# The second half of one transformer layer put into one written order, from the last output projection group to the final norm

## The chip, the cores and the metric

One core of a Trainium2 chip runs the whole kernel in one launch. The metric is the device time of one execution in microseconds (us); less is better. All data are fp32, and a product of high accuracy is made from three products of split operands.

## What is computed

One layer of a diffusion backbone over 512 latent tokens and 256 context tokens with 2048 features. Only the parts around the change matter here. `mod_x` gives six vectors per feature (shift, scale and gate for each of the two blocks):

```python
x = x + g1 * (_merge_heads(o_da, o_mla, subln_w[l], lambda_init) @ w_o[l])
h2 = _modulate(_rmsnorm(x, norm2_w[l]), sh2, s2)
x = x + g2 * _conv_ffn(h2, w_up[l], conv_w[l], conv_b[l], w_down[l])
...
return _rmsnorm(x, final_w)

def _conv_ffn(h, w_up, conv_w, conv_b, w_down):
    g, u = jnp.split(h @ w_up, 2, axis=-1)
    T = g.shape[1]
    gp = jnp.pad(g, ((0, 0), (pad, pad), (0, 0)))
    g = sum(gp[:, j:j + T] * conv_w[j] for j in range(CONV_W)) + conv_b
    return (jax.nn.silu(g) * u) @ w_down
```

## The kernel before

Activations lie with features on the 128 partitions and the 512 tokens along the free dimension: 16 tiles of 128 features. Every operand is split into a high part (cast on ACT) and a low part (raw minus high, on DVE); `mm3` makes a product from three matmuls (L101). A weight block is 128 x 1024 floats: its raw tile `wr` is loaded from the SyncE queue, its high part is `wh`, its low part `wl`, three buffers each.

**Output projection** (L690 to L715). Four groups `g` of four feature tiles, eight weight blocks each, 24 matmuls of 512 columns per block. The 16 products that give the gate of the second block (`next_gemv`) are issued in the groups 1 to 3. After a group DVE adds the residual (L711), the sum `x1` goes to memory from the POOL queue (L714), ACT squares it and POOL adds the squares up in `ss` (L673, L674) for all but the last four tiles.

**Second norm and first two tiles** (L735 to L796). `token_norm` sums the squares over the partitions with matmuls against ones (L680, L684), takes the logarithm and the exponential (L159, L160) and four DVE operations (L161 to L164). Then `first_pair` makes two gate and two up tiles in eight jobs of two feature tiles: `normed` scales a tile (L747), ACT adds the shift per token half (L751), DVE makes the low half (L752). `classical` uses each half on its own: 48 matmuls of 256 columns per weight block. Beside this, `sums` (L756 to L773) makes four sums of quadrants on DVE and splits each into high and low for the later products. This stage has no order written by hand: a scheduler places its operations in each engine's list.

**Third tile, Strassen products and output blocks** (L878 to L1065). From here on the order of PE, ACT, DVE and SyncE is the order of the program (`manual_schedule`). The list `jobs` holds four jobs `u` for the third tile, then seven products `p` per later tile, with the output blocks `d` between them; a job casts and splits the block two jobs ahead. Weight blocks come through two `Ring` objects of three buffers (`wr` and `rb`); a ring issues the next load when a buffer's last use is written.

**Last output block and final norm** (L1069 to L1085). Again placed by the scheduler: for each token half the last four tiles of the activation are multiplied with eight weight blocks (`down`), 24 matmuls of 256 columns each; DVE adds the residual (L843), ACT squares, POOL adds up. When both halves are done, each half has its `token_norm`, then 16 scales on DVE (L1084) and 16 stores from the SyncE queue (L1085).

Of the kernel before, what the change touches and what calls it, by code (L numbers as in the profile page):

```python
# [17 lines left out]
P = 128  # L18
# [34 lines left out]
def layer_kernel(ctx: ExitStack, tc: tile.TileContext, small, rope, c_row, cc_row, x_t, ctx_t, ada, ada_k,  # L53
# [601 lines left out]
    HT = T // 2  # L655
# [20 lines left out]
    def token_norm(pool, ss, last):  # L676

        n = ss.shape[1]
        po = b_tile()[:, :n]
        pe.matmul(po, ones32, ss, start=True, stop=False)  # L680
        for i, x in enumerate(last):
            q = pool.tile([P, T], F32, tag="h", name=nm("sq"), bufs=5)[:, :n]
            sc.square(q, x)
            pe.matmul(po, ones32, q, start=False, stop=i == len(last) - 1)  # L684
        r = pool.tile([P, T], F32, tag="nr", name=nm("nr"), bufs=1)[:, :n]
        t1, t2 = (pool.tile([P, T], F32, tag="h", name=nm("n"), bufs=5)[:, :n] for _ in range(2))
        rstd(r, po, D, t1, t2)
        return r

    x1, ss = [], wo.tile([P, T], F32, name="ss")  # L690
    gv = iter([80 + i for i in range(16)])
    for g in range(4):
# [5 lines left out]
        for kb in range(8):  # L698
            if g and kb % 4 != 3:
                next_gemv(wo, 1)  # L700
            wh, wl = wblock(w_o[g, kb])
            order = [(j, i) for j in range(2) for i in range(4)]
            for j, i in sorted(order, key=lambda t: t[1]) if kb == 7 else order:
                kt, o = kb * 2 + j, j * 512 + i * P
                mm3(outs[i], (wh[:, o:o + P], wl[:, o:o + P]), osp[kt], kt == 0, kt == 15)
        for i in range(4):
            dt = g * 4 + i
            xr = wo.tile([P, T], F32, tag="xr", name=nm("xr"), bufs=3)
            nc.sync.dma_start(xr, x_t[dt])
            x = b2k()  # L710
            ve.scalar_tensor_tensor(out=x, in0=outs[i], scalar=modx[:, 32 + dt:33 + dt], in1=xr,  # L711
                                    op0=ALU.mult, op1=ALU.add)
            x1.append(x)
            gp.dma_start(x1_d[dt], x)  # L714
            if g < 3:  # L715
                add_square(wo, ss, x, dt == 0)
    for dt in range(KT):
        ve.scalar_tensor_tensor(out=a2[:, dt:dt + 1], in0=modx[:, 64 + dt:65 + dt], scalar=1.0,
                                in1=col("n2", dt), op0=ALU.add, op1=ALU.mult)
    db = sm.tile([P, 8], F32, name="db")  # L720
    ve.tensor_tensor(db, modx[:, 56:64], modx[:, 48:56], op=ALU.add)
    wo.release()
    ps_b.release()
    ps_s.release()
    nb[0] = 3
    ps_b = ctx.enter_context(tc.tile_pool(name="ps_m", bufs=4, space=PSUM, reuse_waits="tile"))
# [5 lines left out]
    ff = tc.alloc_tile_pool(name="ff", bufs=1, reuse_waits="tile")  # L732
    hp = tc.alloc_tile_pool(name="hp", bufs=1, side="right", reuse_waits="tile")
    h0, h1 = slice(0, HT), slice(HT, T)
    r = token_norm(hp, ss, x1[12:])  # L735

    def half(t):
        return t[:, h0], t[:, h1]


    hf, hx, t1, t2, t3, t4 = ([None] * KT for _ in range(6))

    def normed(kt):

        b = modx[:, 48 + kt:49 + kt]
        h = hf[kt] = hp.tile([P, T], F32, tag="h", name=nm("h"), bufs=5)
        ve.scalar_tensor_tensor(out=h, in0=x1[kt], scalar=a2[:, kt:kt + 1], in1=r, op0=ALU.mult, op1=ALU.mult)  # L747
        hx[kt] = (a2k(F32R), a2k(F32R) if kt >= 8 else hp.tile([P, T], F32R, tag="h12", name=nm("h12"), bufs=8))
# [31 lines left out]
    def first_pair():  # L780
# [13 lines left out]
        for j in (6, 7):  # L794
            sums(j)
# [374 lines left out]
```

## Time and profile before

| | |
|---|---|
| three runs, us | 2471.26, 2473.78, 2473.87 (median 2473.78) |
| the profiled execution, us | 2470.59 |
| its span, first to last instruction, us | 2468.8 |
| mean granted clock of PE | 0.987 |
| busy share of PE, weight loads, DVE, ACT, POOL | 97%, 81%, 70%, 45%, 10% |
| the chain that ended last | PE 75%, DVE 14%, DMA 4%, ACT 4%, issue 3%, POOL 1% |

The table tells where the time of the whole span lies; a stage may have another limit than the span. In a timeline a line has its start, its length in us, the engine, the line of the program, the operation, output and inputs by name, and the count of merged instructions; in brackets stands how long the engine was idle before it and what ended that. SPq is the SyncE queue, which issues loads and stores. A matmul's length is longer than the distance to the next one, since matmuls overlap.

### The profile page before, as it was taken

Reading aid. Unit: us, or ns where it says so; the run is one execution under the profiler, and the core shown is the slowest. Engines: PE = TensorE matmul, PEld = TensorE weight load, DVE = VectorE, ACT = ScalarE, POOL = GpSimd, SP = SyncE. Lnnn points to the kernel's source line nnn. Section 1 sums busy time; section 2 is a strip of 40 time slices with the busy share of each in tenths; the row PEclk is TensorE's granted clock in tenths of the full one; section 3 lists DMA queues with packets and bytes.
Section 4 is the critical chain, followed back from the end, with each engine's and each line's share of the span. In section 5 each row is a group of like instructions: output and inputs, shape, how many; then the busy total and the mean of one; then the engine's idle time right before and its main releaser. Section 6 shows DMA issues by size and latency. Waiting matters only on the chain.

```text
span 2468.8 us, 33004 instructions
## 1 busy us (share of the span) xinstructions
PE 2388.4 (97%) x12796; PEld 1987.7 (81%) x12796; DVE 1731.8 (70%) x2274; ACT 1117.2 (45%) x1668; POOL 243.4 (10%) x266
## 2 busy tenths in 40 slices
PE   7999999999999999999999999999999999999996
PEld 3778878777677778888888888888888888888886
DVE  4668786398968777387676767675757575757576
ACT  4343121165645542254454545454545454545443
POOL 0000000121200002100101010101010101010113
PEclk8999999999999999999999999999999999999998
DMA  7868889554411158423656465655555555555664
GB/s 274 282 226 307 323 329 321 195 153 131 123 58 43 44 210 314 137 82 119 146 128 146 129 144 130 144 131 142 132 142 135 139 135 139 135 138 136 137 180 145
DMA packets 131859, 407.51 MB, mean 165 GB/s; under 512 B 14451, under 2 KB 25203, under 8 KB 123251
## 3 DMA queue, kind: packets, MB, share of 16 engines
q1 hardware_dynamic: 106422, 356.11, 44.5%
q0 software_dynamic: 25280, 49.30, 11.5%
q8 instruction: 100, 1.64, 0.3%
q14 instruction: 57, 0.47, 0.1%
HBM read 335.88 MB, written 69.48 MB: 164 GB/s over the span
## 4 chain that ended last, share of the span: by engine, by line
PE 75%; DVE 14%; DMA 4%; ACT 4%; issue 3%; POOL 1%; SPq 0%; ACTq 0%; DVEq 0%; POOLq 0%
PE y L981 9%; PE b L104 9%; PE b L105 9%; PE b L106 9%; PE z L981 5%; PE y L982 5%; PE s L104 3%; PE s L105 3%; PE s L106 3%; DMA ada<-in_ada 3%; DVE wl L957 3%; PE s L482 3%; PE z L982 2%; PE x L981 2%; ACT wh L951 1%
## 5 line engine op out<-in xcount | busy, mean ns | idle before, releaser
L104 PE MATMUL b<-ah,wh 128*128 128x512 f32 (+1 forms) x768 | 288.1, 376 | 3.9 <-ACT ah L823 3.9
L105 PE MATMUL b<-al,wh 128*128 128x512 f32 (+1 forms) x768 | 287.0, 374 | 0.0
L106 PE MATMUL b<-ah,wl 128*128 128x512 f32 (+1 forms) x768 | 287.0, 374 | 0.0
L1001 POOL DMA_DIRECT2D x_d<-xs x160 | 139.7, 1004 | 1173.4 <-ACT xs L1000 1171.4
L80 ACT CAST wh<-wr 128x1024 fp32r<-128x1024 f32 (+2 forms) x134 | 132.5, 989 | 269.6 <-PE b L106 78.6
L957 DVE TENSOR_TENSOR wl<-wr,wh 128x1024 fp32r<-128x1024 f32 x125 | 152.7, 1222 | 116.1 <-ACT wh L951 116.1
L981 PE MATMUL y<-a2k,wh 128*128 128x512 f32 x656 | 233.6, 398 | 0.0
L951 ACT CAST wh<-wr 128x1024 fp32r<-128x1024 f32 x125 | 131.3, 1051 | 216.0 <-PE b L105 85.9
L957 DVE TENSOR_TENSOR wl<-rb,wh 128x1024 fp32r<-128x1024 f32 x123 | 150.2, 1222 | 110.6 <-ACT wh L951 110.3
L957 DVE TENSOR_TENSOR wl<-ws,wh 128x1024 fp32r<-128x1024 f32 x123 | 150.2, 1221 | 109.5 <-ACT wh L951 109.4
L81 DVE TENSOR_TENSOR wl<-wr,wh 128x1024 fp32r<-128x1024 f32 (+2 forms) x134 | 155.9, 1164 | 100.9 <-ACT wh L80 97.3
L951 ACT CAST wh<-rb 128x1024 fp32r<-128x1024 f32 x123 | 129.4, 1052 | 203.2 <-PE b L105 58.4
L951 ACT CAST wh<-ws 128x1024 fp32r<-128x1024 f32 x123 | 128.9, 1048 | 154.6 <-DVE ws L925 65.8
L171 DVE CUSTOM_DVE_ANT_0 ada<-ada,cb,smt 128x2048 f32<-128x2048 f32 x64 | 150.6, 2354 | 64.1 <-DMA ada<-in_ada 64.0
L982 PE MATMUL y<-a2k,wl 128*128 128x256 f32 x656 | 183.9, 280 | 0.0
L104 PEld LDWEIGHTS b<-ah,wh 128*128 128x128 f32 x768 | 145.6, 190 | 30.4 <-ACT ah L823 4.1
L106 PEld LDWEIGHTS b<-ah,wl 128*128 128x128 f32 x768 | 145.8, 190 | 26.7
L105 PEld LDWEIGHTS b<-al,wh 128*128 128x128 f32 x768 | 146.0, 190 | 22.6
L981 PE MATMUL y<-b2k,wh 128*128 128x512 f32 x410 | 148.1, 398 | 0.0
L981 PEld LDWEIGHTS y<-a2k,wh 128*128 128x128 f32 x656 | 123.2, 188 | 30.4
L104 PE MATMUL b<-a2k,wh 128*128 128x512 f32 (+1 forms) x376 | 139.8, 374 | 6.6 <-ACT a2k L751 5.0
L105 PE MATMUL b<-a2k,wh 128*128 128x512 f32 (+1 forms) x376 | 140.4, 374 | 0.4 <-DVE a2k L752 0.4
(368 smaller groups left out, 6111.7 us busy)
## 6 DMA issues: line engine op xcount, KB each, us to landing
ada<-in_ada SPq DMA_DIRECT2D x64, 1024.0 KB, 7.0
rb<-in_w_up SPq DMA_DIRECT2D x123, 512.0 KB, 4.5
wr<-in_w_dn SPq DMA_DIRECT2D x96, 512.0 KB, 4.2
x_d<-xs POOLq DMA_DIRECT2D x160, 256.0 KB, 6.0
wr<-in_w_up SPq DMA_DIRECT2D x53, 512.0 KB, 4.1
wr<-in_w_f SPq DMA_DIRECT2D x34, 512.0 KB, 6.9
adak<-in_ada_k SPq DMA_DIRECT2D x32, 512.0 KB, 6.2
ada<-in_ada SPq DMA_DIRECT2D x32, 512.0 KB, 6.4
```

The costliest lines, as they stand in the source:

```text
L80: sc.copy(dst_h, src)
L81: ve.tensor_tensor(dst_l, src, dst_h.bitcast(F32), op=ALU.subtract)
L104: pe.matmul(out, st[0], mv[0], start=start, stop=False, **kw)
L105: pe.matmul(out, st[0], mv[1], start=False, stop=False, **kw)
L106: pe.matmul(out, st[1], mv[0], start=False, stop=stop, **kw)
L171: ve.tensor_tensor_reduce(out=junk, in0=w, in1=vec, op0=ALU.mult, op1=ALU.add, scale=1.0, scalar=col("b_ada", j), accum_out=dst[:, j:j + 1])
L482: pe.matmul(s[:, c0:c1], a, b[:, c0:c1], start=i == 0, stop=i == len(mms) - 1)
L951: sc.copy(hi, raw)
L957: ve.tensor_tensor(lo, raw, hi.bitcast(F32), op=ALU.subtract)
L981: pe.matmul(o, w[j][0], hs[j], start=start and j == 0, stop=False, skip_group_check=True)
L982: pe.matmul(o[:, h0], w[j][1], hs[j][:, h0], start=False, stop=j == 7, skip_group_check=True)
L1001: gp.dma_start(x1_d[dt], x, accum_op=ALU.add)
```

## The change

The order written by hand now begins at the last of the four groups of the output projection and ends with the last store. `jobs` gets eight jobs `o` (last group), eight jobs `n` (the first two tiles) in front and sixteen jobs `f` (last output block, two token halves) behind; all weight blocks but those of `rb` come through one ring.

In `last_projection` the last group's four tiles end one after the other; three of the five sum matmuls stand between the projection's matmuls, and the norm's chain runs by token halves. In `first_tiles` PE takes both feature tiles of a block for the first token half, then for the second; the next block's two tiles are scaled, then the block two ahead is cast and split; every second job POOL forms the quadrant sums in place (four adds per pair of tiles), and ACT and DVE split them at once, in front of the next job's work. `after` issues what `act_after` and `vec_after` issued. In the last stage the two first blocks leave out the last activation tile until it is there; the residual is loaded in one go after the last product; the first half's norm runs beside the second half's matmuls, and in the second half's scaling every third tile goes over ACT and POOL.

```diff
--- before.py
+++ after.py
-    def token_norm(pool, ss, last):
...
+    def residual(dt):
+        xr = wo.tile([P, T], F32, tag="xr", name=nm("xr"), bufs=4)
+        nc.sync.dma_start(xr, x_t[dt])
+        x1.append(b2k())
+        return xr
+    def gated(dt, po, xr, c=slice(0, T)):
+        ve.scalar_tensor_tensor(out=x1[dt][:, c], in0=po[:, c], scalar=modx[:, 32 + dt:33 + dt], in1=xr[:, c],
+                                op0=ALU.mult, op1=ALU.add)
-    for g in range(4):
+    for g in range(3):
...
-            if g and kb % 4 != 3:
+            if g:
                 next_gemv(wo, 1)
...
+    KBS = [kb for j in range(4) for kb in (j, j + 4)]
+    jobs = [("o", kb) for kb in range(8)] + [("n", kb) for kb in KBS] + [("u", b) for b in range(4)]
+    for ft in range(3, NFT):
+        for k in range(7):
+            jobs.append(("p", ft, k))
+            c, n_ = ft // FC, (ft % FC) * 7 + k
+            if c and n_ in DOWN_AFTER:
+                jobs.append(("d", c - 1, DOWN_AFTER.index(n_)))
+    jobs += [("f", th, dp) for th in range(2) for dp in range(8)]
...
+    def high_low(t, src, b=None):
+        hh, hl = half(t)
+        if b is None:
+            sc.copy(hh, src)
+            ve.tensor_tensor(hl, src, hh.bitcast(F32), op=ALU.subtract)
+        else:
+            sc.activation(hh, src, AF.Identity, bias=b)
+            ve.scalar_tensor_tensor(out=hl, in0=src, scalar=b, in1=hh.bitcast(F32), op0=ALU.add, op1=ALU.subtract)
+    def norm_tiles(kt):
+        hf[kt] = mem["hp"].tile([P, T], F32, tag="h", name=nm("h"), bufs=6)
+        hx[kt] = (a2k(F32R), a2k(F32R) if kt >= 8 else mem["hp"].tile([P, T], F32R, tag="h12", name=nm("h12"), bufs=8))
+    def normed(kt, cs=(slice(0, T),)):
+        for c in cs:
+            ve.scalar_tensor_tensor(out=hf[kt][:, c], in0=x1[kt][:, c], scalar=a2[:, kt:kt + 1], in1=mem["r"][:, c],
+                                    op0=ALU.mult, op1=ALU.mult)
+            for t, s in zip(hx[kt], halves):
+                if c.start <= s.start < c.stop:
+                    high_low(t, hf[kt][:, s], modx[:, 48 + kt:49 + kt])
+    def sums(j):
+        a, c = hf[j], hf[j + 8]
+        t1[j] = a2k(F32R)
+        for t in (t3, t2, t4):
+            t[j] = spare.pop(0) if spare else b2k(F32R)
+        d1, d2, d3, d4 = c[:, h1], a[:, h0], a[:, h1], c[:, h0]
+        gp.tensor_tensor(out=d1, in0=c[:, h1], in1=a[:, h1], op=ALU.add)
+        gp.tensor_tensor(out=d3, in0=a[:, h0], in1=a[:, h1], op=ALU.subtract)
+        gp.tensor_tensor(out=d2, in0=d1, in1=a[:, h0], op=ALU.subtract)
+        gp.tensor_tensor(out=d4, in0=c[:, h0], in1=d2, op=ALU.subtract)
+        return [lambda: high_low(t1[j], d1, db[:, j:j + 1]), lambda: high_low(t3[j], d3),
+                lambda: high_low(t2[j], d2, modx[:, 56 + j:57 + j]), lambda: high_low(t4[j], d4)]
...
+    def last_projection(i):
+        kb, w = jobs[i][1], ready[i]
+        if kb < 6:
+            for j in range(2):
+                for d in range(4):
+                    project(live["o"], d, kb * 2 + j, w)
+            cast(i + 2)
+            low(i + 2)
+            return
+        outs, xr = live["o"], live["xr"]
+        def both(d, kbs=(6, 7)):
+            for k in kbs:
+                for kt in (2 * k, 2 * k + 1):
+                    project(outs, d, kt, ready[i - kb + k])
+        def square(src, c=slice(0, T)):
+            if c.start == 0:
+                live["q"] = wo.tile([P, T], F32, tag="sq", name=nm("sq"), bufs=2)
+            sc.square(live["q"][:, c], src[:, c])
+            return live["q"]
+        def put(d):
+            gated(12 + d, outs[d], xr[d])
+            gp.dma_start(x1_d[12 + d], x1[12 + d])
+            return square(x1[12 + d])
+        if kb == 6:
+            both(0)
+            both(1)
+            cast(i + 2)
+            low(i + 2)
+            live["q0"] = put(0)
+            return
+        s = s_tile()
+        po = s[:, :T]
+        both(2)
+        q1 = put(1)
+        pe.matmul(po, ones32, ss, start=True, stop=False, skip_group_check=True)
+        pe.matmul(po, ones32, live["q0"], start=False, stop=False, skip_group_check=True)
+        both(3, (6,))
+        pe.matmul(po, ones32, q1, start=False, stop=False, skip_group_check=True)
+        both(3, (7,))
+        q2 = put(2)
+        pe.matmul(po, ones32, q2, start=False, stop=False, skip_group_check=True)
+        for c in halves:
+            gated(15, outs[3], xr[3], c)
+            q3 = square(x1[15], c)
+            pe.matmul(po[:, c], ones32, q3[:, c], start=False, stop=True, skip_group_check=True)
+        gp.dma_start(x1_d[15], x1[15])
+        wo.release()
+        hp = mem["hp"] = tc.alloc_tile_pool(name="hp", bufs=1, side="right", reuse_waits="tile")
+        r = mem["r"] = hp.tile([P, T], F32, name="nr")
+        n1, n2 = (hp.tile([P, T], F32, tag="h", name=nm("n"), bufs=6) for _ in range(2))
+        for c in halves:
+            sc.activation(r[:, c], po[:, c], AF.Ln, bias=epst, scale=1.0 / D)
+            sc.activation(r[:, c], r[:, c], AF.Exp, scale=-0.5)
+            ve.tensor_scalar(out=n1[:, c], in0=po[:, c], scalar1=1.0 / D, scalar2=EPS, op0=ALU.mult, op1=ALU.add)
+        norm_tiles(0)
+        norm_tiles(1)
+        for c in halves:
+            ve.scalar_tensor_tensor(out=n2[:, c], in0=r[:, c], scalar=-0.5, in1=r[:, c], op0=ALU.mult, op1=ALU.mult)
+            ve.tensor_tensor(n2[:, c], n2[:, c], n1[:, c], op=ALU.mult)
+            ve.scalar_tensor_tensor(out=r[:, c], in0=n2[:, c], scalar=1.5, in1=r[:, c], op0=ALU.add, op1=ALU.mult)
+            for kt in (0, 1):
+                normed(kt, (c,))
+        cast(i + 2)
+        low(i + 2)
+    queue = []
+    def first_tiles(i):
+        kb, n_ = jobs[i][1], KBS.index(jobs[i][1])
+        w = weights(i)
+        if n_ == 0:
+            live["n"] = [b_tile(*t) for t in (("b", 3), ("b", 3), ("x", 1), ("b", 3))]
+        for c in range(2):
+            for j in range(2):
+                for d in range(4):
+                    classical(live["n"][d], kb * 2 + j, w[j * 4 + d], n_ == 0 and j == 0, n_ == 7 and j == 1, (c,))
+        if n_ < 7:
+            for j in range(2):
+                norm_tiles(KBS[n_ + 1] * 2 + j)
+                normed(KBS[n_ + 1] * 2 + j)
+        cast(i + 2)
+        low(i + 2)
+        if n_ % 2:
+            for j in (n_ - 1, n_):
+                queue.extend(sums(j))
+        while queue and n_ < 7:
+            queue.pop(0)()
+    def third_tile(i):
+        b, w = jobs[i][1], weights(i)
+        if b == 0:
+            live["s"] = [b_tile(g_, 2) for g_ in "yz"]
+        for j in range(8):
+            kt = (b % 2) * 8 + j
+            classical(live["s"][b // 2], kt, w[j], kt == 0, kt == KT - 1)
+        while queue:
+            queue.pop(0)()
+        if b == 2:
+            mem["hp"].release()
+            mem["mm"] = tc.alloc_tile_pool(name="mm", bufs=1, side="right", reuse_waits="tile")
+            mem["rb"] = Ring(mem["mm"], "rb", 3, items_b)
+        if b == 3:
+            weight_sum(3, 1)
+        cast(i + 2)
+        low(i + 2)
+        if b < 2:
+            acts[b] = activate(b, live["n"][2 * b], live["n"][2 * b + 1])
...
-        def act_after(i):
...
-        def vec_after(i):
...
+    def after(job):
...
+    def load_residual():
+        for dt in range(KT):
+            x1[dt] = b2k()
+            nc.sync.dma_start(x1[dt], x1_d[dt])
+    rest = []
+    def last_output(i):
+        th, dp = jobs[i][1:]
+        c, n_ = halves[th], th * 8 + dp
+        outs = live.setdefault("f", {})
+        def part(i, fs):
+            w, dp = weights(i), jobs[i][2]
+            for d in range(2):
+                dt = dp * 2 + d
+                if 0 in fs:
+                    outs[dt] = b_tile() if dp != 1 or th else b_tile("xyz"[d], (1, 2)[d])
+                for f in fs:
+                    mm3(outs[dt][:, h0], w[f * 2 + d], [a[:, c] for a in acts[NFT - FC + f]], f == 0, f == FC - 1)
+        if n_ == 0:
+            part(0 + i, (0, 1, 2))
+            part(1 + i, (0, 1, 2))
+            after(jobs[i - 1])
+            v = live[NFT - 1]
+            silu(convolve(NFT - 1, v["g"], v["t"]))
+            acts[NFT - 1] = finish(v["t"], multiply(v["t"], v["u"]))
+            exp_ln_tables()
+        elif n_ == 1:
+            part(i - 1, (3,))
+            part(i, (3,))
+        else:
+            part(i, (0, 1, 2, 3))
+        if n_ == 10:
+            norm_sum(0)
+        cast(i + 2)
+        if n_ > 1:
+            add(n_ - 1 if n_ > 2 else 0)
+            if n_ == 2:
+                add(1)
+        low(i + 2)
+        if n_ == 11:
+            norm_scale(0)
+        if n_ > 11:
+            for _ in range(2 if n_ < 14 else 6):
+                if rest:
+                    rest.pop(0)()
+        if n_ == 15:
+            add(15)
+            norm_sum(1)
+            norm_scale(1)
+            while rest:
+                rest.pop(0)()
...
+    def norm_sum(th):
+        po = live["po", th] = b_tile("y", 2)[:, :HT]
+        for i, q in enumerate((live["ss", th], live["q", th, 0], live["q", th, 1])):
+            pe.matmul(po, ones32, q, start=i == 0, stop=i == 2)
+    def norm_scale(th):
+        r, n1, n2 = fin(), fin(), fin()
+        rstd(r, live["po", th], D, n1, n2)
+        for dt in range(KT):
+            x = x1[dt][:, halves[th]]
+            def scaled(dt=dt, x=x):
+                if th and dt % 3 == 2:
+                    y = fin()
+                    sc.mul(y, x, col("fw", dt))
+                    gp.tensor_tensor(out=y, in0=y, in1=r, op=ALU.mult)
+                else:
+                    y = x
+                    ve.scalar_tensor_tensor(out=y, in0=x, scalar=col("fw", dt), in1=r, op0=ALU.mult, op1=ALU.mult)
+                nc.sync.dma_start(out_t[dt][:, halves[th]], y)
+            rest.append(scaled)
...
+        mem["ra"] = Ring(wp, "wr", 3, items_a)
+        live["o"] = [b_tile() for _ in range(4)]
+        live["xr"] = [residual(12 + d) for d in range(4)]
+        for i in range(2):
+            cast(i)
+            low(i)
         for i, job in enumerate(jobs):
...
+            {"o": last_projection, "n": first_tiles, "u": third_tile, "p": strassen, "d": strassen,
+             "f": last_output}[job[0]](i)
```

## Rows read from the trace of the kernel before

**Rows 1.** The page, busy us, share of the span and instructions of each engine.

```profile
PE 2388.4 (97%) x12796; PEld 1987.7 (81%) x12796; DVE 1731.8 (70%) x2274; ACT 1117.2 (45%) x1668; POOL 243.4 (10%) x266
```

**Rows 2.** Windows, first two tiles: length, each engine's busy time, clock, DMA share, GB/s.

```profile
1080.00:1090.00 10.00, 10.00 (x86) 10.00 (x85) 9.89 (x21) 5.99 (x13) 0.00 (x0) 1.00 0.34 105
```

**Rows 3.** Timeline of PE, from the last projection matmul to the first Strassen product.

```profile
1051.33 0.40 PE L106 MATMUL b<-a2k,wl 128*128 128x512 f32 x1
...
1053.15 3.70 PE L684 MATMUL b<-sq,ones 128*128 128x512 f32 x8 [0.57 <-ACT sq L683]
...
1061.88 0.80 PE L104 MATMUL b<-a2k,wh 128*128 128x256 f32 x2 [5.03 <-ACT a2k L751]
...
1130.98 0.39 PE L104 MATMUL z<-a2k,wh 128*128 128x256 f32 x1 [2.64 <-ACT wh L951]
...
1132.62 0.42 PE L104 MATMUL z<-a2k,wh 128*128 128x256 f32 x1
...
1138.17 0.39 PE L106 MATMUL z<-a2k,wl 128*128 128x256 f32 x1
...
1140.56 0.40 PE L981 MATMUL y<-a2k,wh 128*128 128x512 f32 x1
```

**Rows 4.** Waits of the SyncE queue: waited for, us in total, times, longest.

```profile
SPq L868 <- DVE d L771: 23.0, 1, 23.0
```

**Rows 5.** Timeline of PE, last output block: first, first after the wait, last.

```profile
2391.65 0.28 PE L104 MATMUL b<-ah,wh 128*128 128x256 f32 x1
...
2398.95 1.01 PE L104 MATMUL b<-ah,wh 128*128 128x256 f32 x3 [3.90 <-ACT ah L823]
...
2444.40 0.28 PE L106 MATMUL b<-ah,wl 128*128 128x256 f32 x1
```

**Rows 6.** Timeline of DVE and ACT: the first tile, and the final norm's half.

```profile
1060.53 1.41 DVE L747 SCALAR_TENSOR_TENSOR h<-b2k,a,nr 128x512 f32<-128x512 f32 x2
1061.32 0.51 ACT L751 ACTIVATE a2k<-h,modx 128x256 fp32r<-128x256 f32 x1 [3.08 <-DVE h L747]
...
1061.86 0.48 DVE L752 SCALAR_TENSOR_TENSOR a2k<-h,modx,a2k 128x256 fp32r<-128x256 f32 x1
...
2446.87 0.47 ACT L159 ACTIVATE nr<-b,epst 128x256 f32<-128x256 f32 x1 [6.87 <-PE b L684]
...
2449.21 6.42 DVE L1084 SCALAR_TENSOR_TENSOR b2k<-a2k,smt,nr 128x256 f32<-128x256 f32 x16
```

**Rows 7.** Timeline of ACT and DVE: cast and split of one weight block, low halves of sums.

```profile
1046.09 1.05 ACT L80 CAST wh<-wr 128x1024 fp32r<-128x1024 f32 x1 [4.38 <-PE b L105]
...
1047.17 1.23 DVE L81 TENSOR_TENSOR wl<-wr,wh 128x1024 fp32r<-128x1024 f32 x1 [4.22 <-ACT wh L80]
...
1113.48 0.76 DVE L81 TENSOR_TENSOR b2k<-d,b2k 128x256 fp32r<-128x256 f32 x2
```

**Rows 8.** Timelines of POOL and DVE where adds and weight splits meet or don't.

```profile
2407.14 0.74 POOL L674 TENSOR_TENSOR ss<-ss,sq 128x256 f32<-128x256 f32 x1 [0.44 <-ACT sq L673]
...
2404.88 1.23 DVE L81 TENSOR_TENSOR wl<-wr,wh 128x1024 fp32r<-128x1024 f32 x1 [0.38 <-ACT wh L80]
...
2405.31 1.39 POOL L674 TENSOR_TENSOR ss<-ss,sq 128x256 f32<-128x256 f32 x1 [0.89 <-ACT sq L673]
...
975.40 1.30 POOL L674 TENSOR_TENSOR ss<-ss,sq 128x512 f32<-128x512 f32 x1
...
976.09 1.71 DVE L81 TENSOR_TENSOR wl<-wr,wh 128x1024 fp32r<-128x1024 f32 x1 [1.70 <-ACT wh L80]
```

**Rows 9.** Timeline of ACT: the last gate's operation, and the table load of the final norm.

```profile
2394.41 0.82 ACT L805 ACTIVATE t<-g,smt 128x512 f32<-128x512 f32 x1 [1.36 <-DVE g L1024]
...
2437.70 1.28 ACT L155 ACT_TABLE_LOAD   x1
```

**Rows 10.** Line 1085, the stores: shortest, median, longest ns; us to landing.

```profile
L1085 SPq DMA_DIRECT2D out_t<-b2k x32: 332/408/461, 2449.7 to 2466.0; - x32
...
DMA to landing us min/median/max: 1.7/1.8/2.0
```

More of the change, by code (lines that the diff above doesn't have):

```diff
@@ L720, in layer_kernel @@
[L720 to L748, printed above, removed]
-        for t, c in zip(hx[kt], (h0, h1)):
-            hh, hl = half(t)
-            sc.activation(hh, h[:, c], AF.Identity, bias=b)
-            ve.scalar_tensor_tensor(out=hl, in0=h[:, c], scalar=b, in1=hh.bitcast(F32), op0=ALU.add, op1=ALU.subtract)
@@ L854, in layer_kernel @@
+    items_a, items_b = [], []
+    for job in jobs:
+        if job[0] != "p":
+            items_a.append((job, sources[job[0]](*job[1:]), 1))
+        elif job[2] == 0:
+            ft = job[1]
+            items_a.append((("w11", ft), w_up[ft - 2, 0, 0], 2))
+            items_b += [(("w12", ft), w_up[ft - 2, 1, 0], 2), (("w21", ft), w_up[ft - 2, 0, 1], 2),
+                        (("w22", ft), w_up[ft - 2, 1, 1], 3)]
     class Ring:
@@ new lines, in classical, with activate, gate_in @@
+    def classical(out, kt, w, start, stop, cs=(0, 1)):
+        for i in cs:
+            mm3(out[:, halves[i]], w, half(hx[kt][i]), start and i == 0, stop and i == 1, True)
+    def activate(ft, g, u):
+        t = silu(convolve(ft, g, gate_in(ft, g)))
+        return finish(t, multiply(t, u))
+    def gate_in(ft, g):
+        t = mem["ff"].tile([P, T], F32, tag="t", name=nm("t"), bufs=1)
+        sc.activation(t, g, AF.Identity, scale=col("cw", NFT + ft), bias=col("cb", ft))
+        return t
@@ new lines, in operand, with cast @@
+    def operand(job):
+        ra = mem["ra"]
+        if job[0] != "p":
+            return ra.tiles[job], lambda: ra.used(job)
+        ft, k = job[1:]
+        if k == 0:
+            return ra.tiles["w11", ft], lambda: ra.used(("w11", ft))
+        if k in (2, 3, 6):
+            return sums_[ft, 1 if k == 3 else 2], None
+        key = ({1: "w21", 4: "w12", 5: "w22"}[k], ft)
+        return mem["rb"].tiles[key], lambda: mem["rb"].used(key)
+    def cast(i):
+        if i < last:
+            raw, done = operand(jobs[i])
+            hi, lo = (wp.tile([P, 1024], F32R, tag=g, name=nm(g), bufs=3) for g in ("wh", "wl"))
+            sc.copy(hi, raw)
+            ready[i] = hi, lo, raw, done
```

471 lines of the change are left out of this document (177 added, 294 removed).

## The prediction

> **What bounds the kernel now.** I read the page's busy times first: TensorE (PE) is busy for 97% of the span [rows 1]. The whole change can therefore win back no more than the places where PE stands still or runs at the lower clock, so I looked for those next, in the stretches of ten microseconds after the output projection. One of them, twenty microseconds after the second norm, shows the opposite of what I looked for: PE is busy for all of it and VectorE (DVE) for 9.89 of 10 [rows 2]. A matmul of 256 columns, 0.28 long and counted at both edges, begins there every (10 + 0.28)/86 = 0.12 us. DVE works there at PE's own pace; it has nothing to spare.
>
> Then the timeline of PE alone. The last matmul of the output projection starts at 1051.33 and ends about 0.22 later; call that end E. The first matmul of the up projection starts at 1061.88, 10.3 us after E, and waits 5.03 for ScalarE (ACT). At 1130.98 PE waits again, 2.64, for a weight block, and from 1132.62 to 1138.17 it starts 27 matmuls 0.213 apart, which is the 1.2 GHz level after the 0.12 of the 2.4 GHz level. The first Strassen product starts at 1140.56, 89.0 after E [rows 3]. The late wait comes from the SyncE queue: its loads stood 23.0 us behind the three `rb` loads, whose memory DVE was still reading [rows 4]. The last output block starts at 2391.65, loses 3.90 to the last `ah`, ends at 2444.52 [rows 5], and the remaining 24.3 us to the end of the span are the final norm. So from the last product to the end the kernel needs 77.2 us.
>
> **The change part by part.** Between the first and the last Strassen product the list of instructions is the same (the merged `after` issues what `act_after` and `vec_after` issued, in the same order): 0. The modulation products of the output projection move into its second and third group; both versions load 16 of them beside PE work, so I take 0 there too.
>
> *From E to the first product.* Three of the five sum matmuls go in front of E. Eight records of such sums take 3.70, two per matmul, 0.93 each [rows 3]: E comes 2.8 later. Behind it now stands a chain in token halves. Add and square of 256 columns (0.48 and about 0.4) and half a sum (0.46) end at 1.5. From the logarithm to the first scale the final norm's half takes 2.34 now (2446.87 to 2449.21) [rows 6]; here the second half's logarithm and exponential (0.47 and about 0.4) stand in between: 4.8. Scale 0.48, bias 0.50 [rows 6], and the first matmul starts at E + 5.9 instead of 10.3. What is late next is DVE. In the written order a feature tile is scale, bias (ACT), low half, bias, low half, and DVE can't start anything else while it waits. From the scale's start to the first low half 1.33 pass (1060.53 to 1061.86), each low half takes some 0.40 more (0.48 less its overlap) [rows 6]: 2.13 per tile, of which 0.67 is waiting. Before, two scales run back to back there. A job has two tiles, then the next weight block: its cast of 1.05 follows the last bias, so DVE waits 0.57 more, then 1.13 for the low half (1.22 less its overlap) [rows 7]. That is 2 x 2.13 + 1.70 = 5.96 per job against PE's 48 x 0.12 = 5.76. Every second job has eight more low halves of the sums, four of 0.39 and four of 0.34 (two of these take 0.76 with their overlap) [rows 7]: 2.92. A pair of jobs so costs DVE 14.84 and PE 11.52. The sums no longer wait for a gap, as they did: they stand in front of the next tiles, for which PE waits.
>
> The adds that made these sums move from DVE to GpSimd (POOL), eight per pair. One takes 0.74 alone, but 1.39 when a weight split of DVE ran from before its start (2404.88 to 2406.11): it ended 0.59 after the split. The other way round a split that started in a POOL add took 1.71 instead of 1.22 [rows 8]. So 8 x 0.59 = 4.7 us of POOL's work can't lie beside DVE's. The ends: all of it falls in DVE's own waits of 3.8 per pair (pair 14.84), or none (pair 19.6). I take 2.0 of the 4.7 on the path, 16.85, since POOL only finds a wait free after the operation in front of it has finished. The Trainium skill (SBUF — State Buffer, Who interferes with whom) says that a vector instruction with two SBUF inputs and a GpSimd instruction that reads SBUF exclude each other, and the later one fully blocks; the rows agree for one meeting, none shows a queue of eight. By that rule with every add meeting an operation the pair is 19.6 and the sum below rises by 8.1; by the 2.0 taken above it stands.
>
> Job by job: DVE is through both halves of the first two tiles and one weight block at 13.7 (four half tiles of 1.43, three operations, 1.8 for the block, from 4.8), the next job's second tile is split at 17.7, 35 matmuls of that job remain (4.2): the second job ends at 21.9. Three pairs: 21.9 + 50.6 = 72.4. Then the third tile, 4 x 5.76 = 23.0: here the loads are written well ahead, and the `rb` loads stand behind the last tile's reads only, so the wait of 2.64 and the low clock behind it go. First product at 95.5, plus 2.8 in front: 98.3 against 89.0, a **loss of 9.3**. The earlier start and the third tile's wait, about 2 and 6, are in that; the vector-bound pairs eat them.
>
> *From the last product to the end.* 384 matmuls of 0.12 are 46.1. In front of the last `ah` stand now 36 matmuls (4.3) and a chain of 5.4: copy and sum of 256 columns 0.9, then from the gate's operation at 2394.41 to PE at 2398.95 the 4.54 of now [rows 5, 9]. PE waits 1.1, 0.6 more for `al`, and 1.3 for the next block, whose cast follows a table load of 1.28 [rows 9]. With 1.4 for the first half's sums the last matmul ends at 50.5, before 52.9. The 16 loads of the residual now stand in front of the fifth weight block on SyncE's queue; that block is used 15 us later, so 0. Then the tail. In the last five jobs DVE has 15.8 us of work (ten adds 3.9, three splits 3.4, the first half's norm 2.2, 16 scales 6.3) and POOL 10 adds of 0.59 beside it: between 1.4 (all hidden) and 7.3 (none) more than PE's 14.4; I take 5.2. Add, square, two sums and the norm's chain take 3.9 more: the second half's factor is there at 9.0. Eleven scales on DVE (0.40 each, 16 in 6.42 [rows 6]) and five on POOL (0.59), excluding each other, are 7.3; some three issues of 0.41 and 1.8 of landing remain [rows 10]: 19.7 where 24.3 stood. Together 70.2 against 77.2: a **gain of 7.0**.
>
> **The sum** is +9.3 - 7.0 = +2.3. The profiled execution took 2470.6 and its span 2468.8; it lies 3.2 under the median of the three runs, 2473.8. On the median: 2476.1. About 0.2% (4.9 us) is what a measurement of this kernel can tell from no change, so this is no change.
>
> **The rivals.** *The adds on POOL cost nothing*, because they fit DVE's waits. Then the pairs are 14.84 (6.1 less), and the tail has DVE free at 1.1 and the scales side by side: 13.9 instead of 19.7. Sum -9.7: 2464.1, faster. For it: 3.8 of waits per pair, nearly the 4.7. Against it: the split of 1.71, where POOL held DVE up.
>
> *PE falls to the lower clock in the vector-bound jobs.* Each pair leaves PE standing for about 2 us in one piece and again for 0.3 to 1.3 in others. Before, the clock fell after 2.64 of standing and 0.7 more, and 27 matmuls ran at 0.213 before it rose [rows 3]. A job then takes 48 x 0.213 = 10.2, more than DVE's 8.4, so PE itself sets the pace: six jobs, 1.8 each, 10.8 in all. Sum +13: 2487, slower. It decides from the point where gaps of 2 us are enough; gaps of 0.57 behind the projection were not [rows 3].
>
> *The list is not kept as written*, and DVE is filled as before. Then the jobs run at PE's pace from the first one's end at 14.1: eleven times 5.76 more make 77.5, 80.3 with the sums in front, a gain of 8.7 instead of the loss. Sum -15.7: 2458. Nothing in the rows speaks for it.
>
> **How the numbers follow.** The forecast has 0.50, the first rival 0.30, the second 0.17, the third 0.03. The range takes in nearly all of the first rival and the contention's upper bound (part of the way to +10.4): 2463 to 2483. Faster: the first rival without its upper edge and the third, 0.29. Slower: the second, and the forecast's upper edge, 0.22. Within 0.2%: 0.49.
>
> **What would show it.** Right: PE's first job starts 6 us after the projection, DVE is busy or waiting for ACT through all eight jobs, PE waits about 2 us before the fourth, sixth and eighth, POOL adds of well over 0.74, no wait for a load in the third tile, 1 to 3 us of standing at the last output, a last scale about 16 us after the last weight matmul. Wrong: PE without waits in the jobs, adds of 0.74 throughout, or a tail under 15.

## The result: slower by 0.4%, and the profile after

Six runs of the changed kernel took 2481.29 to 2487.21 us, median 2482.4; six of the kernel before on the same chip 2471.26 to 2473.87, median 2473.21. The ratio is 1.0041, 95% interval 1.0029 to 1.0054: slower by 9.2 us, 7 more than the forecast's +2.3 and just inside its range (2463 to 2483). The profiled execution took 2481.29, its span 2479.5.

The page still has PE busy for 97%, and POOL for 12% instead of 10% [rows 1]:

```profile
PE 2394.3 (97%) x12790; PEld 1989.6 (80%) x12790; DVE 1740.5 (70%) x2244; ACT 1121.5 (45%) x1676; POOL 287.9 (12%) x307
```

The timeline of PE, where rows 3 and 5 were read: the last projection matmul and the sums, the up projection's start, the fourth, sixth and eighth job of its first two tiles, the first product, the last output's first matmul, its waits, its end.

```profile
1053.76 0.40 PE L106 MATMUL b<-a2k,wl 128*128 128x512 f32 x1
...
1055.18 1.13 PE L967 MATMUL s<-sq,ones 128*128 128x256 f32 x4 [0.17 <-ACT sq L938]
1060.61 0.58 PE L104 MATMUL b<-a2k,wh 128*128 128x256 f32 x1 [4.30 <-ACT a2k L790]
...
1086.46 0.38 PE L104 MATMUL b<-a2k,wh 128*128 128x256 f32 x1 [1.75 <-ACT a2k L790]
...
1103.15 0.38 PE L104 MATMUL b<-a2k,wh 128*128 128x256 f32 x1 [1.74 <-ACT a2k L790]
...
1119.84 0.38 PE L104 MATMUL b<-a2k,wh 128*128 128x256 f32 x1 [1.76 <-ACT a2k L790]
...
1150.99 0.40 PE L1042 MATMUL y<-a2k,wh 128*128 128x512 f32 x1
...
2402.22 0.28 PE L104 MATMUL b<-ah,wh 128*128 128x256 f32 x1
...
2411.45 0.39 PE L106 MATMUL b<-ah,wl 128*128 128x256 f32 x1 [0.76 <-DVE wl L910]
2419.25 0.58 PE L104 MATMUL b<-ah,wh 128*128 128x256 f32 x1 [3.13 <-DVE b2k L1179]
...
2458.80 0.39 PE L104 MATMUL b<-ah,wh 128*128 128x256 f32 x1 [1.00 <-DVE b2k L1179]
...
2460.21 0.28 PE L106 MATMUL b<-ah,wl 128*128 128x256 f32 x1
```

These lines divide what follows into four stretches. From the projection's end (E, 1051.55 before, 1053.99 now) to the first product: 89.0 before, 97.0 now, and E itself 2.4 later. The products: 1251.1 and 1251.2. The last output, first to last weight matmul: 52.9 [rows 5] and 58.1. The tail after it: 24.3 and 19.2. So 10.4 were lost up to the first product (8.0 in the stretch, 2.4 in front of it), and in the last two together nothing was won: the tail gives 5.1, the last output takes 5.2.

What stands behind the 3.13 is seen in the other queues. SyncE's timeline (SPq), then ACT's, then DVE's:

```profile
2399.92 9.52 SPq L1117 DMA_DIRECT2D b2k<-x_d  x16
2409.77 9.39 SPq L767 DMA_DIRECT2D wr<-in_w_dn  x4
...
2416.50 1.04 ACT L904 CAST wh<-wr 128x1024 fp32r<-128x1024 f32 x1 [5.42 <-DMA wr<-in_w_dn]
...
2417.58 1.22 DVE L910 TENSOR_TENSOR wl<-wr,wh 128x1024 fp32r<-128x1024 f32 x1 [3.48 <-ACT wh L904]
2418.72 0.87 DVE L1179 SCALAR_TENSOR_TENSOR b2k<-b,modx,b2k 128x256 f32<-128x256 f32 x2
```

Read it backwards. PE waits for a PSUM bank that the add of 2418.72 frees. That add has its operands, but stands on DVE behind the low half of the fifth block; that waits for the cast, the cast for the load, and the load was issued at 2409.77, behind sixteen loads whose issue took 9.5. The releaser's name (an add of L1179) tells only the last link.

### The profile page after: what moved, and what is told of

Same layout as the page of the kernel before. It is cut to its first block, busy times and chain, and to the rows that moved or that the text cites. A ratio compares the mean times of both kernels' runs of the same rounds, so it can differ in the third digit from the quotient of the medians.

```text
span 2479.5 us, 33003 instructions
## 1 busy us (share of the span) xinstructions
PE 2394.3 (97%) x12790; PEld 1989.6 (80%) x12790; DVE 1740.5 (70%) x2244; ACT 1121.5 (45%) x1676; POOL 287.9 (12%) x307
## 4 chain that ended last, share of the span: by engine, by line
PE 81%; DVE 11%; ACT 4%; issue 2%; DMA 1%; POOL 1%; SPq 0%; DVEq 0%; ACTq 0%; POOLq 0%
PE y L1042 10%; PE b L104 10%; PE b L105 10%; PE b L106 10%; PE z L1042 5%; PE y L1043 5%; PE s L104 3%; PE s L105 3%; PE s L106 3%; PE z L1043 3%; PE s L482 3%; PE x L1042 2%; DVE wl L910 2%; ACT wh L904 1%; PE x L1043 1%
## 5 line engine op out<-in xcount | busy, mean ns | idle before, releaser
L910 DVE TENSOR_TENSOR wl<-wr,wh 128x1024 fp32r<-128x1024 f32 x157 | 195.2, 1244 | 154.7 <-ACT wh L904 154.7
L904 ACT CAST wh<-wr 128x1024 fp32r<-128x1024 f32 x157 | 164.6, 1049 | 263.2 <-PE b L105 108.3
L80 ACT CAST wh<-wr 128x1024 fp32r<-128x1024 f32 (+3 forms) x102 | 99.1, 971 | 217.7 <-PE b L106 68.2
L81 DVE TENSOR_TENSOR wl<-wr,wh 128x1024 fp32r<-128x1024 f32 (+3 forms) x102 | 116.9, 1146 | 59.7 <-ACT wh L80 56.1
L104 PE MATMUL b<-a2k,wh 128*128 128x512 f32 (+1 forms) x376 | 144.3, 384 | 13.3 <-ACT a2k L790 11.6
L105 PE MATMUL b<-a2k,wh 128*128 128x512 f32 (+1 forms) x376 | 143.4, 381 | 1.2
```

Of the source, the lines that this page charges most:

```text
L80: sc.copy(dst_h, src)
L81: ve.tensor_tensor(dst_l, src, dst_h.bitcast(F32), op=ALU.subtract)
L104: pe.matmul(out, st[0], mv[0], start=start, stop=False, **kw)
L105: pe.matmul(out, st[0], mv[1], start=False, stop=False, **kw)
L904: sc.copy(hi, raw)
L910: ve.tensor_tensor(lo, raw, hi.bitcast(F32), op=ALU.subtract)
```

## The experiments

The twelve profiles of the experiments differ by up to 6.6 us in when the norm's half sums begin (1054.02 to 1060.61), before anything in which they differ. So I compare by stretch. "Sums" is from that start to the first product, "last output" from its first to its last weight matmul, "tail" from there to the end; "ratio" is to the kernel before, over all runs.

| kernel | sums | products | last output | tail | median us | ratio, 95% interval |
|---|---|---|---|---|---|---|
| changed | 95.8 | 1251.2 | 58.1 | 19.2 | 2482.40 | 1.0041, 1.0029 to 1.0054 |
| e1 weights first | 95.5 | 1251.5 | 57.5 | 18.2 | 2479.61 | 1.0039, 1.0028 to 1.005 |
| e2 no additions | 88.9 | 1250.9 | 57.0 | 19.2 | 2476.89 | 1.0016, 1.0004 to 1.0027 |
| e3 scales first | 88.8 | 1251.0 | 58.4 | 19.2 | 2473.62 | 1.0008, 0.9996 to 1.0019 |
| e4 additions on DVE | 100.0 | 1250.9 | 57.3 | 19.2 | 2485.30 | 1.0054, 1.0031 to 1.0076 |
| e5 tail on DVE | 95.7 | 1250.9 | 58.0 | 18.2 | 2482.81 | 1.0042, 1.0028 to 1.0055 |
| e6 early residual | 95.6 | 1251.7 | 53.7 | 19.1 | 2476.40 | 1.0019, 1.0007 to 1.003 |
| e7 adds before scales | 95.5 | 1250.5 | 58.4 | 16.2 | 2478.70 | 1.0031, 1.0021 to 1.0042 |
| e8 four edits | 91.1 | 1251.0 | 54.5 | 16.2 | 2472.00 | 1.0002, 0.9992 to 1.0012 |
| e9 three edits | 88.7 | 1251.4 | 54.5 | 16.1 | 2469.47 | 0.9988, 0.9978 to 0.9998 |
| e10 six banks | 88.7 | 1252.0 | 50.7 | 20.8 | 2471.34 | 0.9995, 0.9983 to 1.0007 |
| e11 scales ahead | 88.8 | 1252.3 | 50.7 | 20.8 | 2470.50 | 0.9993, 0.9983 to 1.0002 |
| e12 lighter tail | 88.8 | 1254.3 | 54.5 | 15.3 | 2468.61 | 0.9990, 0.9981 to 0.9999 |

**e1: the weight blocks ahead of the residual.**

```diff
-                if ft == NFT - 1:
-                    load_residual()
...
+        if job == ("p", NFT - 1, 6):
+            load_residual(0)
...
+        if n_ < 3:
+            load_residual(n_ + 1)
```

> The changed kernel with the 16 loads of the residual issued four at a time behind the weight blocks of the last output, instead of all sixteen ahead of the fifth block. Theory (the sixteen issues, 9.5 us on SyncE, and their bytes hold the fifth block up; PE's 3.13 before that block, the part of a standing just before it and the low clock follow from this): the fifth block is issued about 2 us after the last product ends its vector work instead of 9.8, lands 3.5 to 4 after, no cast waits over 1 us for a weight block, the f stage (last product to last weight matmul) falls from 58.1 to between 50.5 and 53, and the span by 5 to 8 us, to 2472 to 2475. Rival (the releaser that the profile names, the DVE adds of the last output that free PSUM, are late by themselves): the fifth block lands earlier, but PE still waits 2 to 4 us for the adds in the second block; f stage 56 to 58, span 2478 to 2480.

The wait of 3.13 went, the last output won 0.7, and so neither theory held as written. DVE's and PE's timelines show what came in its place:

```profile
2416.30 0.49 DVE L1181 SCALAR_TENSOR_TENSOR b2k<-b,modx,b2k 128x256 f32<-128x256 f32 x1 [0.96 <-DMA b2k<-x_d]
...
2418.94 0.48 DVE L1181 SCALAR_TENSOR_TENSOR b2k<-b,modx,b2k 128x256 f32<-128x256 f32 x1 [0.48 <-DMA b2k<-x_d]
...
2422.95 0.39 PE L104 MATMUL b<-ah,wh 128*128 128x256 f32 x1 [1.29 <-DVE b2k L1181]
```

The adds now wait for the residual itself, the next blocks land late too, and PE waits four times instead of once. The place in the queue is not the whole cause: 4 MB more have to come within the same 15 us.

**e6: the same loads 17 us sooner.** The operands of the first two products get the tiles that are reused first, so that the residual can go there; the last output's scratch tiles take the other pool in exchange.

```diff
+            if ft == NFT - 1 and k == 2:
+                load_residual()
...
-            x1[dt] = b2k()
+            x1[dt] = a2k()
```

> The changed kernel with the 16 loads of the residual some 14 us earlier: before the third of the last seven Strassen products, into tiles of the other pool (a2k) whose last readers are the first two products; the scratch tiles of the last output take the b2k pool in exchange. Issuing four at a time behind the weight blocks won only 0.7 of the f stage, because the waits went on to the loads themselves and to the next blocks. Theory (4 MB of residual and the weight blocks want the DMA queues in the same 15 us): with the residual there before the stage, no wait for a load in it; f stage 51 to 53 instead of 58.1 (46.1 of matmuls, 2.4 of standing at the last gate's output, 1.4 of sums, 1.5 of VectorE's backlog at the end), span 5 to 7 us less than the changed kernel's for equal time ahead of it. Rival (VectorE's adds are late by themselves, and free PSUM late): PE still waits 2 to 4 us for the adds after the second block, f stage 55 to 58.

SyncE's timeline, the last output's first and last matmul, and two stretches of windows (length, busy PE, PEld, DVE, ACT, POOL, clock, DMA share, GB/s):

```profile
2382.16 9.49 SPq L1119 DMA_DIRECT2D a2k<-x_d  x16
...
2401.40 0.28 PE L104 MATMUL b<-ah,wh 128*128 128x256 f32 x1
...
2454.99 0.28 PE L106 MATMUL b<-ah,wl 128*128 128x256 f32 x1
...
2415.00:2420.00 5.00, 5.00 (x42) 4.79 (x41) 4.26 (x8) 2.92 (x7) 4.69 (x5) 1.00 0.69 202
2420.00:2425.00 5.00, 5.00 (x44) 5.00 (x44) 4.05 (x5) 3.19 (x6) 4.55 (x5) 1.00 0.65 198
```

The same windows of the changed kernel:

```profile
2415.00:2420.00 5.00, 1.87 (x13) 1.66 (x12) 2.26 (x4) 3.50 (x8) 1.67 (x2) 0.88 0.51 191
2420.00:2425.00 5.00, 5.00 (x36) 5.00 (x35) 4.01 (x5) 2.02 (x5) 4.68 (x5) 0.78 0.64 203
```

58.1 became 53.7. The 4.4 are two things in the changed kernel: 3.3 of standing (a matmul at 2415.84, the next at 2419.25) and 1.1 of the 1.2 GHz level after it (twelve matmuls 0.213 apart instead of 0.12). Both are gone, so the loads in this stage are shown as their cause, and the rival (adds late by themselves) falls. The stretch is 0.7 over the theory's 51 to 53.

**e2, e4: GpSimd's additions.** e2 leaves the four lines out, e4 has `ve` for `gp` in them (the first of the four):

```diff
-        gp.tensor_tensor(out=d1, in0=c[:, h1], in1=a[:, h1], op=ALU.add)
+        ve.tensor_tensor(out=d1, in0=c[:, h1], in1=a[:, h1], op=ALU.add)
```

> The changed kernel without GpSimd's 32 quadrant additions and subtractions: the sums' high and low parts are taken of the quadrants themselves, so the five Strassen operands that are sums hold other values; everything else is issued as before. Theory (GpSimd and VectorE shut each other out): the pair of up-projection jobs falls from 16.7 to 14.8 (the sum of VectorE's own work in the written order), end of output projection to first product from 97.0 to 90 to 92.5, span 2473 to 2475. Rival (the additions fit VectorE's waits for ScalarE and cost nothing; the order alone sets the pair): pair 16.3 to 16.7, span 2478 to 2480. Second rival (PE's lower clock in these jobs sets the pair): waits of PE go down, the clock stays below 0.8 in the same stretches and the pair stays above 16.

> The changed kernel with the 32 quadrant additions issued on VectorE instead of GpSimd, at the same place of the program. An operation of this shape on VectorE is about 0.34 to 0.42, eight per pair 2.7 to 3.4. Theory (VectorE bounds the pair, and GpSimd's additions already cost it about 2 per pair): the two nearly cancel, pair 17.3 to 18.2 (14.84 plus 2.7 to 3.4), span 2480 to 2484. Rival (GpSimd's additions cost VectorE nothing): pair 19.4 to 20.1, span 2488 to 2491. Rival (moving the additions to VectorE costs less than the shutting out): pair under 16.7, span under 2479.

PE's waits before the fourth and sixth job, without the additions and with them on DVE:

```profile
1088.67 0.38 PE L104 MATMUL b<-a2k,wh 128*128 128x256 f32 x1 [1.75 <-ACT a2k L790]
1103.45 0.38 PE L104 MATMUL b<-a2k,wh 128*128 128x256 f32 x1 [0.78 <-ACT a2k L790]
```

```profile
1088.08 0.58 PE L104 MATMUL b<-a2k,wh 128*128 128x256 f32 x1 [5.17 <-ACT a2k L790]
...
1106.29 0.38 PE L104 MATMUL b<-a2k,wh 128*128 128x256 f32 x1 [3.53 <-ACT a2k L790]
```

A pair of jobs takes 16.7 in the changed kernel, 14.8 without the additions (1103.45 - 1088.67) and 18.2 with them on DVE. So on POOL they cost 1.9 per pair, on DVE 3.4 (eight of 0.42). The first theory holds in both, in e4 at the upper edge of its range; the two rivals (they cost nothing; the clock sets the pair) fall. DVE's timelines show where the 1.9 lie, a scale and a low half in the changed kernel and then the same two in e2:

```profile
1091.52 1.22 DVE L800 SCALAR_TENSOR_TENSOR h<-b2k,a,nr 128x512 f32<-128x512 f32 x1
...
1093.72 0.96 DVE L791 SCALAR_TENSOR_TENSOR h<-h,modx,h 128x256 fp32r<-128x256 f32 x1
```

```profile
1093.25 0.75 DVE L800 SCALAR_TENSOR_TENSOR h<-b2k,a,nr 128x512 f32<-128x512 f32 x1
...
1094.98 0.48 DVE L791 SCALAR_TENSOR_TENSOR h<-h,modx,h 128x256 fp32r<-128x256 f32 x1
```

Five DVE operations of a pair are some 0.47 longer beside the additions, 2.4 in all, and DVE's waits for ACT fall from 3.2 to 2.75: 1.9 more.

**e3, e8, e11: other orders on DVE.** e3 issues both scales of a job ahead of the parts; e8 also moves the cast; e11, built on e10 (see below), scales the tiles of the job after next and issues the additions in the even jobs.

```diff
...
+            for kt in kts:
+                norm_tiles(kt)
+                scale(kt, slice(0, T))
+            for kt in kts:
+                for t, s in zip(hx[kt], halves):
+                    high_low(t, hf[kt][:, s], modx[:, 48 + kt:49 + kt])
```

> The changed kernel with the two scales of a job's tiles issued back to back on VectorE ahead of the eight high and low parts, so that VectorE has work while ScalarE makes the first bias form. Theory (the written order leaves VectorE waiting for ScalarE 0.57 per tile and more): VectorE wins 0.6 to 1.3 per job, the pair falls from 16.7 by 1.2 to 2.6, to 14.1 to 15.5, and the span by 4 to 8 us, to 2471 to 2476; GpSimd's additions then find fewer free places and eat some of it. Rival (GpSimd's additions run in those very waits, so the time goes to them whatever the order): pair 16.3 to 16.9, span 2478 to 2481.

> The kernel with six banks, and in the up projection the scales of the job after next ahead of the block's low half (even jobs) or behind the sums' parts (odd jobs), so that VectorE has work while ScalarE casts. Theory (VectorE's waits for the cast, 0.57 each, and for the first bias are what is left to win): pair from 14.95 to 13.8 to 14.4, sums to first product 86 to 88. Rival (GpSimd's additions run in VectorE's waits): pair 14.7 or more, 88.5 or more, as moving the cast alone made it 15.5.

e3's pair takes 14.95 and the sums' stretch falls by 7.0. PE's first matmuls of the fourth and sixth job, and DVE's timeline between them, in which no line has a wait:

```profile
1084.95 0.38 PE L104 MATMUL b<-a2k,wh 128*128 128x256 f32 x1 [1.69 <-ACT a2k L790]
...
1099.90 0.38 PE L104 MATMUL b<-a2k,wh 128*128 128x256 f32 x1 [1.70 <-ACT a2k L790]
...
1087.07 1.70 DVE L913 TENSOR_TENSOR wl<-wr,wh 128x1024 fp32r<-128x1024 f32 x1
1088.70 2.38 DVE L798 SCALAR_TENSOR_TENSOR h<-b2k,a,nr 128x512 f32<-128x512 f32 x2
1091.00 0.95 DVE L791 SCALAR_TENSOR_TENSOR a2k<-h,modx,a2k 128x256 fp32r<-128x256 f32 x1
...
1094.51 1.21 DVE L913 TENSOR_TENSOR wl<-wr,wh 128x1024 fp32r<-128x1024 f32 x1
...
1098.57 1.40 DVE L798 SCALAR_TENSOR_TENSOR h<-b2k,a,nr 128x512 f32<-128x512 f32 x2
1099.90 0.47 DVE L791 SCALAR_TENSOR_TENSOR a2k<-h,modx,a2k 128x256 fp32r<-128x256 f32 x1
```

The last three lines are the price of block, scales and low half without POOL at work, the first three beside its additions: 0.5, 1.0 and 0.5 more, the last four times over. That is some 3.4 per pair, where the waits of the changed kernel had left 1.9 to pay. So e11, which gives DVE work ahead in another way, has a pair of 14.97, and its rival holds. POOL's and DVE's timelines there show how they take turns:

```profile
1094.48 0.81 POOL L820 TENSOR_TENSOR h<-h,h 128x256 f32<-128x256 f32 x1
1095.37 0.80 POOL L821 TENSOR_TENSOR h<-h,h 128x256 f32<-128x256 f32 x1
...
1094.61 0.96 DVE L791 SCALAR_TENSOR_TENSOR a2k<-h,modx,a2k 128x256 fp32r<-128x256 f32 x1
1095.50 0.95 DVE L791 SCALAR_TENSOR_TENSOR h<-h,modx,h 128x256 fp32r<-128x256 f32 x1
```

e8's pair is 15.5, outside both of its theories: its earlier cast makes the second tile's bias forms late, and DVE waits 0.86 for them.

**e5, e7: the tail.** e5 gives POOL's five scales to DVE; e7 spreads the first half's scales 4, 4, 4, 4 and puts the last adds ahead of the last four.

```diff
-            for _ in range(2 if n_ < 14 else 6):
-                if rest:
-                    rest.pop(0)()
+            if n_ == 15:
+                add(15)
+                norm_sum(1)
+            for _ in range(4):
+                rest.pop(0)()
```

> The changed kernel with all 16 scales of the second half of the final norm on VectorE, none on ScalarE and GpSimd. Theory (GpSimd's five multiplications and VectorE's eleven shut each other out: the eleven took 6.78, 0.62 each, where the kernel before took 0.40 each): sixteen alone take 6.4, the tail (last weight matmul to the end) stays at 18.5 to 19.3. Rival (0.62 is what such an operation costs here, whoever else works): sixteen take 9.9, the tail is 22 to 22.5 and the span 3 us longer.

> The changed kernel with the first half's 16 scales spread four to each of the last four jobs (instead of 2, 2, 6, 6), and in the last job the adds and sums of the last tiles ahead of the four scales. Theory (VectorE's backlog of written scales holds up the adds that free PSUM, 1.5 us of PE's waits, and the last add by 2.0 after the last weight matmul): f stage 57 to 57.7, the last add starts within 0.3 of the last weight matmul's end, tail 16.7 to 17.7 instead of 19.2, span 2.5 to 3.5 less. Rival (the scales left over then stand in the second half's chain and give it back): tail 18.7 to 19.5.

The last scales on DVE, in the changed kernel and in e5:

```profile
2468.01 6.78 DVE L1208 SCALAR_TENSOR_TENSOR b2k<-b2k,smt,a2k 128x256 f32<-128x256 f32 x11
```

```profile
2470.32 6.42 DVE L1208 SCALAR_TENSOR_TENSOR b2k<-b2k,smt,a2k 128x256 f32<-128x256 f32 x16
```

Sixteen alone take less than eleven beside POOL's five: POOL's help is worth less than nothing (tail 18.2, a little under the expected range). From the first of these scales to the end it is 11.5 in the changed kernel, 10.7 in e5 and in e12. e1's tail of 18.2 has another reason: its last four sum matmuls took 1.13 at a granted clock of 1.00, where the changed kernel's took 2.08 at 0.53. e7's tail is 16.2, better than expected, but its last output is 0.3 longer instead of shorter: PE still waits for banks.

**e8, e9, e10, e12: edits together.** e9 is e3, e6 and e7 in one kernel, e8 has the moved cast besides; e10 adds three banks to e9:

```diff
-                    outs[dt] = b_tile() if dp != 1 or th else b_tile("xyz"[d], (1, 2)[d])
+                    tag = "b" if n == 0 else "xy"[d] if n == 1 else "bzbzbx"[(n * 2 + d - 4) % 6]
```

e12 is e9 with e5's scales, the first half's norm one job sooner and its scales three to a job.

> Four edits together: the early residual, the two scales of a job's tiles back to back, the next block's cast on ScalarE behind the first tile's bias forms instead of behind the second's (so that VectorE need not wait for it before the block's low half), and the last adds ahead of the spread scales. Theory: VectorE's pair is 6 of scales and lows, 2.3 for two blocks, 2.9 for the sums' low halves and 2.0 of GpSimd's shutting out, 13.2 to 13.9 instead of 16.7; sums of the norm to first product 95.8 to 86 to 88; f stage 51 to 53, tail 17 to 17.7; span 2460 to 2465, faster than the kernel before by 0.2 to 0.4%. Rival (VectorE's waits that the cast leaves were GpSimd's places, so GpSimd takes them back): pair 14.7 to 15, span 2465 to 2468.

> The early residual, the two scales of a job back to back (the cast left where the changed kernel has it), and the last adds ahead of the spread scales. If the three gains add: sums of the norm to first product 88.7, f stage 53.7 to 54.5, tail 16.2, that is 13 to 14 us under the changed kernel's 95.8 + 58.1 + 19.2, and 2 to 4 under the kernel before. If the scales back to back only win where the other stages are late: 90 to 92 in the first stretch, level with the kernel before.

> The kernel of three edits, with the outputs of the last stage in six PSUM banks instead of three (the y, z and x banks stand empty there). Theory (PE's waits in the last four jobs are for banks that late adds free): no wait for an add, f stage 51.5 to 52.5. Rival (VectorE with GpSimd's shutting out is the bound of the last jobs, so PE only ends earlier): the tail grows by what the f stage wins, their sum stays within 0.5 of the kernel of three edits.

> The kernel of three edits with all scales of the second half on VectorE (alone that took 0.9 off the tail) and the first half's sums and scales one job sooner, three to a job and four in the last. Theory (the end is set by what VectorE and GpSimd together still have to do, and VectorE has idle time one job sooner): the tail falls from 16.1 to about 15.2, the f stage from 54.5 to 53 to 54, 1.4 to 2.4 in all; with equal time ahead of the second norm the median falls to 2467 to 2468. Rival (what is left is the chain of the second half's norm and its sixteen scales): tail and f stage together stay within 0.7 of 70.65.

e9's gains add, and it beats both kernels: 0.12% under the one before, interval 0.02 to 0.22%. e10 gives 3.8 in the last output and loses 4.7 in the tail, where PE's sums wait for POOL's; the sums in e10, then in e9:

```profile
2451.86 2.93 PE L1204 MATMUL y<-b2k,ones 128*128 128x256 f32 x6 [3.77 <-POOL b2k L1197]
```

```profile
2449.93 1.56 PE L1202 MATMUL y<-b2k,ones 128*128 128x256 f32 x6 [0.49 <-POOL b2k L1195]
```

The sum grows by 0.9, more than its rival's 0.5. The six sums explain the difference: behind the 3.77 of standing they take 1.4 more, at a granted clock of 0.50 where e9 has 1.00. Without that the sum would be 0.5 under e9's, as the rival has it: DVE and POOL are the bound there, and banks for the most part only move the wait. e12's tail and last output are 69.9 where e9 has 70.65, 0.8 less: nearer to its rival's 0.7 than to its theory's 1.4. Its median is the lowest, 2468.61, though its products took 3 us longer than e9's. 2.2 of these are lost at the third product: PE waits 1.89 until ACT has read out a bank, where e9 waits 1.18, and the ten matmuls behind it run at the 1.2 GHz level (granted clock 0.80 from 1152 to 1157), in e9 at 1.00. The other 0.7 are within what the column differs by.

## Why the prediction was off, step by step

**What bounds the kernel:** right. DVE's list sets the pace of the first two tiles, and what fills it decides.

**From E to the first product**, forecast +9.3, measured +10.4: right in size and in mechanism. The first matmul starts 6.6 after E (5.9 forecast, from terms that add up to 5.5), PE waits 1.75 before the fourth, sixth and eighth job ("about 2"), the pair is 16.7 (16.85). Its two parts are confirmed on their own: DVE's written order 14.78 (14.84), POOL's additions 1.9 (2.0 taken between 0 and 4.7). That the 2.0 came so near is in part luck: it was a choice within that range, made from eight adds of 0.59, where five meetings of 0.47 less 0.45 of saved waits were measured. In e3, without waits on DVE, the same additions cost 3.4; so in the changed kernel DVE's waits hid a part of it. A low half of 0.47 takes 0.95 beside an add, so the two do exclude each other; but in e11 a low half and an add of 0.80 follow each other every 0.88, in less than the two lengths together. The Trainium skill (SBUF — State Buffer, Who interferes with whom) has the later of two such instructions fully blocked for the whole of the earlier one; these rows show a shorter exclusion. The row behind the working's 0.59 showed it too: an add that takes 0.74 alone ended 0.59 after the split [rows 8]. The wait for a load in the third tile is gone, as said. Not tried was the place of the sums: the kernel before splits its last sums at about 1121, beside the third tile, and no run puts their 2.9 per pair there in the written order.

**From the last product to the end**, forecast -7.0, measured +0.1. The step that failed: "The 16 loads of the residual now stand in front of the fifth weight block on SyncE's queue; that block is used 15 us later, so 0". PE's use was far off indeed (the wait of 3.13 falls in the middle of the fourth block), but the block's cast and low half were written much sooner, and the adds that free PSUM stand behind that low half on DVE. The step took PE for the only one who waits for the block. It also didn't price the issue of sixteen loads, 9.5. This term is 4.4 by e6. Another 3.2 of the last output's 7.6 over the working's 50.5 are left in e6. Nearly all of it, 3.1, are waits for PSUM banks (gaps between matmuls over the usual 0.12), the longest two (0.55 and 1.00) for DVE's adds behind the written scales: the working had put DVE's backlog of 5.2 into the tail alone, while with three banks some of it already stops PE. With six banks (e10) these waits are gone and the last output takes 50.7; there the tail takes 20.8 (19.7), 1.4 of it by the granted clock of 0.50. How the backlog falls on the two in the changed kernel itself is argued from this, not shown apart.

**The tail**, forecast 19.7, measured 19.2: near, but by errors that cancel, which is luck. The second half's factor is there 7.7 after the last weight matmul (9.0 forecast), which fits a part of the backlog having stopped PE before; the eleven scales took 6.78 beside POOL's five (7.3); behind them 4.7 pass to the end, where the terms named were three issues and a landing, 3.0. (The terms named add up to 19.3.)

**The rivals.** *The adds on POOL cost nothing* falls by e2. *PE falls to the lower clock*: it did fall, the granted clock is 0.76 from 1085 to 1090 and 0.69 from 1105 to 1110, after the waits of 1.75. But e2's clock falls too (0.66 from 1090 to 1095), and its pair is DVE's sum to 0.1; the clock did not set the pair, and this rival's 2487 is nearer to the median of 2482.4 than the forecast's 2476 is, for a reason that isn't there. *The list is not kept* falls by the pairs.

## What to carry to other kernels

When a load is delayed, follow its first reader and then everything written behind that reader on its engine's queue; the first use on PE is not the due time. A bulk transfer should be issued where the queue is idle, not merely behind more urgent loads: moving it within the same 15 us won 0.7, moving it 17 us sooner 4.4. Work given to GpSimd beside a full VectorE came back here as longer VectorE operations, 1.9 per pair where VectorE had waits and 3.4 where it had none.

## What the runs showed of the hardware

Two orders of the same DVE work (e3's, which e9, e10 and e12 share, and e11's) end at the same pair, 14.95 and 14.97: with no waits left on DVE, POOL's eight additions cost it 3.4 in both. A DVE operation that meets an addition grows by about 0.48, whatever its own length: in e3 a weight split from 1.21 to 1.70, a low half from 0.47 to 0.95. An issue of one residual load took 0.59 on average on SyncE (9.52 for 16), where stores took 0.41 [rows 10]; behind them the fifth block, issued at 2409.77, was ready 6.7 later.
